# Head sums on quarters of TensorE, fixed orders in the key stage, and matrix exchanges ahead of the weight loads

## The chip, the cores and the metric

The kernel runs on one core of one Trainium2 chip. The metric is the device time of one execution in microseconds (us); lower is better. The figure for a kernel is the median of its runs.

## The reference

The program is a small decoder trunk of two layers: RWKV-7 time mixing, then gated linear attention, each followed by a squared-ReLU MLP. The width is 2048, there are 272 tokens (16 learned ones and 256 of the sequence), and everything is float32. Cut to the part that the change touches, the time mixing computes

```python
xr, xw, xk, xv, xa, xg = (x + xx * mix[i] for i in range(6))   # xx: previous token minus x
r, k, v = xr @ w_rkv[0], xk @ w_rkv[1], xv @ w_rkv[2]
w_log = -softplus(-(w0 + tanh(xw @ w1) @ w2)) - 0.5
a = sigmoid(a0 + (xa @ a1) @ a2)
kk = heads(k * k_k)                                            # 32 heads of 64
kk = kk / max(sqrt(sum(kk * kk, axis=-1)), 1e-12)              # sum over the head
k = k * (1 + (a - 1) * k_a)
decay = exp(-exp(w_log))
y = rwkv7_scan(r, decay, k, v, -kk, kk * a)                    # S <- S diag(w) + (S a) b^T + v k^T
bonus = sum(r * k * r_k, axis=-1) * v                          # sum over the head
```

The scan is carried out in chunks of 64 tokens. Inside a chunk it needs a 64x64 matrix of scores for each head and the inverse of a triangular matrix made from it.

## The kernel before

Activations lie with the 2048 channels on 16 tiles of 128 partitions and the 272 tokens along the free dimension. A projection onto one output tile f (0 to 15) multiplies 16 weight blocks of 128x128 with the 16 input tiles. To keep float32 accuracy, each weight and each input is split into a high and a low part, and a block takes three matmuls (`mm3`, L163 to L165). Weights arrive in half tiles of 128x1024 (`raw`, 512 KB, L132, on the SP queue); ScalarE makes `hi` (L140) and VectorE `lo` (L141). There are three `raw` buffers and two each of `hi` and `lo`. A scheduler orders the instructions of each engine by priority; weight loads are raised by 2000 places, so that they are issued well ahead.

The stages around the change, in the order of the program:

- **Low-rank stage** (`lora`, from L470). For each f it computes two tiles: the running sum of the decay, and a. It stores both (`ca`, 272 KB) in a scratch tensor in DRAM, `cad`.
- **Key stage** (the loop from L567). For each f: the projection `ps`; `ca` is read back; ScalarE makes exp(-) and exp(+) of the decay sum (`W` L574, `iW` L575), `kk` (L576), its square `sq` (L577), and the factor for `kn` (L578). TensorE sums `sq` over each head by a 128x128 matrix of ones on two diagonal blocks (`bones`, L580), ScalarE takes the inverse root (L581, L582), and VectorE makes the tiles `bk` and `ar` of products with W and iW. They go to DRAM (`bkd`, `ard`, 288 KB each). A second product with `bones` (L595) sums `kn` for the bonus, and ScalarE copies the result to `r` (L596). VectorE copies the last decay of each chunk to `WC` (L597) and the column without a decay at the head of each chunk of `ar` (L586). At f = 0 the input tiles of the value projection are mixed (L332 and after) on VectorE.
- **Scores and inversion.** `bk` and `ar` of eight tiles (16 heads) are fetched from DRAM when f is 7. `scores` (L525, and the masks on VectorE into `AM`) is called after f = 10 to 13. The triangular systems are written to DRAM (`sysd`, L531), read back in another layout (`sysA`, L549), inverted by 30 steps of two VectorE operations (`upd`, `sysA`) and four transposes (L561), written out (`invd`, L559), and read into `AM` (L565). The inversion of the first batch starts after f = 13. There are four batches, 0 to 3.
- **Recurrence.** After the key stage the value projection and others run, with the chunk recurrence between them. `merge` (L658) completes the inverses of a batch and needs `AM` from `invd`. Batches 1 to 3 are scored and inverted between these projections, and merged later.
- From about 600 us on the output projections, the MLP and the second layer run, which the change doesn't touch.

Of the kernel before, what the change touches and what calls it, by code (L numbers as in the profile page):

```python
# [11 lines left out]
F32R = mybir.dt.float32r  # L12
# [42 lines left out]
class Kern:  # L55
# [242 lines left out]
    def rwkv(self, done):  # L298
# [171 lines left out]
        def lora(f):  # L470
            l2 = self.t(e2, [96, 2, P], "l2", 3)
            nc.sync.dma_start(l2, ap["lora2"][f])
            st = self.t(ep, [P, 2, T], "ca", 2)
# [22 lines left out]
        Wf = self.t(ep, [P, T + 1], "W")  # L496
        nc.gpsimd.memset(Wf[:, 0:1], 1.0)
        W = Wf[:, 1:]

        def put(dst, slot, a, b, skip=0):  # L500
            v = dst[:, :512].rearrange("q (c s t) -> q c s t", c=4, s=2)[:, :, slot]
            tt(v, a[:, : 4 * C].rearrange("q (c t) -> q c t", c=4), b[:, : 4 * C].rearrange("q (c t) -> q c t", c=4))
            o = 512 + 32 * slot
            tt(dst[:, o + skip : o + 16], a[:, 4 * C + skip :], b[:, 4 * C + skip :])

# [9 lines left out]
        def scores(b, c, e):  # L515
            BK, AR = BKs[c > 1], ARs[c > 1]
            n, np = (C, 4) if c < NC4 else (32, 8)
            o = 128 * (c % 2) if c < NC4 else 256
            cs = slice(o, o + 2 * n)

            pv = [self.ptr().rearrange("p (h m) -> p h m", h=np)[: 2 * n, :, : 2 * n] for _ in range(2)]
            for p in range(np):
                for q in range(2):
                    rows = slice(64 * q, 64 * q + 64)
                    nc.tensor.matmul(pv[q][:, p], BK[rows, 4 * e + p, cs], AR[rows, 4 * e + p, cs], start=True, stop=True)  # L525
            dst, mk = (AMs[c > 1][:, c % 2, 8 * e : 8 * e + 8], self.maskA) if c < NC4 else (AMrs[0], self.maskR)
            for q in range(2):
                tt(dst[:, q::2], pv[q], mk.unsqueeze(1).to_broadcast([2 * n, np, 2 * n]))

            for rows, x in blocks(c, slice(8 * e, 8 * e + 8) if c < NC4 else slice(16)):  # L530
                nc.sync.dma_start(sysd[b][rows].rearrange("h s t -> s h t"), x)  # L531

        def blocks(c, heads):
            if c == NC4:
# [7 lines left out]
        def invert(b):  # L542
            X = sysA
            n = P if b % 2 else 64
            some_rows = [slice(0, 64), slice(96, 112)][: 1 + b % 2]
            if b % 2:
                nc.gpsimd.memset(X[64:96], 0.0)
            for rows in some_rows:
                nc.sync.dma_start(X[rows], sysd[b][rows])  # L549
            nc.gpsimd.memset(X[:n].rearrange("p a b -> p (a b)")[:, ::33], 1.0)  # L550
            yield
            for s in range(1, 31):
                k, m = 31 - s, s
                w = self.t(lp, [P, 256], "upd", 1)[:n, : k * m].rearrange("p (a b) -> p a b", a=m)
                tt(w, X[:n, s : s + 1, s + 1 :].to_broadcast([n, m, k]), X[:n, :m, s : s + 1].to_broadcast([n, m, k]))
                tt(X[:n, :m, s + 1 :], X[:n, :m, s + 1 :], w, ALU.add)
                yield
            for rows in some_rows:
                nc.sync.dma_start(invd[b][rows], X[rows])  # L559
            for k in (slice(8 * i, 8 * i + 8) for i in range(4)):  # L560
                nc.vector.transpose(t11.rearrange("p c h s -> p s c h")[:, k], X[0:32, k])  # L561
                yield
            for c in ((2, 3, 4) if b % 2 else (0, 1)):
                for rows, x in reversed(blocks(c, slice(0, 16))):
                    nc.sync.dma_start(x, invd[b][rows].rearrange("h s t -> s h t"))  # L565

        for f in range(KT):  # L567
            r = rr[f]
            bk, ar = st2[0][f % 2], st2[1][f % 2]
            ps = self.proj(pair(wk, f), xk, T, bank=self.pry if f % 3 == 2 else None)  # L570
            ca = self.t(ep, [P, 2, T], "ca", 2)
            nc.sync.dma_start(ca.rearrange("p a t -> p (a t)"), cad[f])
            iW, kk, sq, kn = (self.t(ep, [P, T], n, 2) for n in ("iW", "kk", "sq", "kn"))
            nc.scalar.activation(W, ca[:, 0], AF.Exp, scale=-DECAY)  # L574
            nc.scalar.activation(iW, ca[:, 0], AF.Exp, scale=DECAY)  # L575
            nc.scalar.mul(self.two(kk), ps, self.vec("k_k", f))  # L576
            nc.scalar.activation(sq, kk, AF.Square)  # L577
            nc.scalar.activation(kn, ca[:, 1], AF.Identity, scale=self.vec("k_a", f), bias=self.omka[:, f : f + 1])  # L578
            ss = self.pm()[:, :T]
            nc.tensor.matmul(ss, self.bones, sq, start=True, stop=True)  # L580
            nc.scalar.activation(sq, ss, AF.Ln, bias=self.tiny)  # L581
            nc.scalar.activation(sq, sq, AF.Exp, scale=-0.5)  # L582
            tt(self.two(kn), ps, self.two(kn))
            nc.vector.scalar_tensor_tensor(out=kk, in0=sq, scalar=1e12, in1=kk, op0=ALU.min, op1=ALU.mult)
            put(ar, 0, kk, Wf[:, :T], 1)
            nc.vector.tensor_copy(ar[:, 0:513:128], kk[:, ::C])  # L586
            tt(kk, kk, ca[:, 1])
            put(bk, 1, kk, iW)
            put(bk, 0, kn, iW)
            nc.sync.dma_start(bkd[f], bk)  # L590
            nc.vector.scalar_tensor_tensor(out=kn, in0=r, scalar=self.vec("r_k", f), in1=kn, op0=ALU.mult, op1=ALU.mult)
            put(ar, 1, r, W)
            nc.sync.dma_start(ard[f], ar)
            rk = self.pu()[:, :T]
            nc.tensor.matmul(rk, self.bones, kn, start=True, stop=True)  # L595
            nc.scalar.copy(r, rk)  # L596
            nc.vector.tensor_copy(WC[:, f], W[:, C - 1 : 4 * C : C])  # L597
            if f == 0:
                xv = mix(3, self.xp)
                early2.close()  # L600
                wl = ExitStack()
                lp = wl.enter_context(tc.tile_pool(name="wl", bufs=1, reuse_waits="tile"))
                BKs, ARs = ([self.t(lp, [P, 8, 256], n)] for n in ("BK0", "AR0"))
                AMs, AMrs = [self.t(lp, [P, 2, 16, 128], "AM0")], []
                sysA = self.t(lp, [P, 32, 32], "sysA")
                t11 = sysA.rearrange("p a b -> p (a b)")[64:96].rearrange("p (c h s) -> p c h s", c=2, h=16)
                nc.gpsimd.memset(sysA, 0.0)
            if f == 7:
                fetch(0, BKs, bkd)
                fetch(0, ARs, ard)  # L610
            if 9 < f < 14:
                scores(0, (f - 10) // 2, f % 2)
            if f == 13:
                inv = invert(0)
            if f > 13:
                for _ in range(6):
                    next(inv, None)
# [4 lines left out]
        BKs.append(self.t(kp, [P, 8, 320], "BK1"))  # L622
# [269 lines left out]
        units1 = ((2, 0), (2, 1), (3, 0), (3, 1), (4, 0))  # L892
        self.split_parts = 2
        for i in ((0, 128), (128, 320)):
            fetch(1, BKs, bkd, i)
            fetch(1, ARs, ard, i)
        ahead()
        with tc.manual_schedule(engines={mybir.EngineType.PE}):
# [423 lines left out]
```

## Time and profile before

| | us |
|---|---|
| median of 3 runs | 2404.45 (2400.09, 2404.45, 2407.26) |
| profiled execution | 2402.54 |
| its span | 2400.8 |
| TensorE busy | 2360.9 |
| VectorE busy | 1611.9 |
| ScalarE busy | 1242.4 |
| GpSimd busy | 6.6 |

The span runs from the first to the last instruction that the profiler saw. Busy is the time in which an engine had an instruction under way; what is missing to the span is idle. A row of a timeline gives the start, the duration, the engine, the line of the program and the operation with its output and input tiles, and in brackets the time for which the engine sat idle and what ended it. A row of a table by windows gives for a stretch of the span the busy time of TensorE, of its weight loads (PEld), VectorE (DVE), ScalarE (ACT) and GpSimd (POOL), then the granted clock of TensorE, the share of the DMA engines and the rate.

### The profile page before, as it was taken

What the parts mean: (1) busy time and instruction counts of PE and PEld (TensorE: products, weight loads), DVE (VectorE), ACT (ScalarE), POOL (GpSimd) and SP (SyncE); (2) the same over time, 40 slices, a digit from 0 to 9 for tenths busy, and PEclk for the clock granted to TensorE, in tenths of its full rate; (3) what the DMA queues carried; (4) which work ended last, traced back from release to release, by engine and by line L of the source; (5) the groups of instructions that cost most, each with busy time, mean ns of one, the idle gap of its engine ahead of it and who ended that gap; (6) DMA issues with size and microseconds to landing.
All of it is one profiled execution on the core that took longest, in us unless ns stands there. A gap on an engine that the chain in (4) does not pass through costs nothing. (4 is left out here: it accounts for less than half of the span.)

```text
span 2400.8 us, 48047 instructions
## 1 busy us (share of the span) xinstructions
PE 2360.9 (98%) x19689; PEld 2244.1 (93%) x19689; DVE 1611.9 (67%) x2734; ACT 1242.4 (52%) x1975; POOL 6.6 (0%) x20
## 2 busy tenths in 40 slices
PE   9999999899999999999999999999999999999998
PEld 8888888889999999999999999999999999999997
DVE  8777886858655555555556777767666666666666
ACT  6376644556555445445345556555555445445444
POOL 0000000000000000000000000000000000000000
PEclk9999999999999999999999999999999999999999
DMA  6578864524555555555555554455555555555554
GB/s 210 169 235 293 248 190 146 146 83 163 183 187 193 187 191 191 188 193 186 192 189 190 196 181 167 159 176 193 182 201 200 200 201 200 202 202 202 201 201 169
DMA packets 160732, 455.34 MB, mean 190 GB/s; under 512 B 34112, under 2 KB 50624, under 8 KB 160512
## 3 DMA queue, kind: packets, MB, share of 16 engines
q1 hardware_dynamic: 160512, 452.27, 55.8%
q8 instruction: 154, 2.52, 0.4%
q14 instruction: 66, 0.54, 0.1%
HBM read 433.86 MB, written 18.35 MB: 188 GB/s over the span
## 5 line engine op out<-in xcount | busy, mean ns | idle before, releaser
L141 DVE TENSOR_TENSOR lo<-raw,hi 128x1024 fp32r<-128x1024 f32 (+1 forms) x818 | 927.4, 1140 | 534.1 <-ACT hi L140 525.9
L140 ACT CAST hi<-raw 128x1024 fp32r<-128x1024 f32 (+1 forms) x818 | 794.6, 979 | 939.4 <-PE pj L164 546.8
L163 PE MATMUL pj<-x,hi 128*128 128x272 f32 (+1 forms) x2624 | 748.6, 285 | 1.7 <-DVE hres L300 1.0
L165 PE MATMUL pj<-x,lo 128*128 128x272 f32 (+1 forms) x2624 | 734.5, 280 | 4.3 <-DVE lo L141 4.1
L164 PE MATMUL pj<-x,hi 128*128 128x272 f32 (+1 forms) x2624 | 734.0, 280 | 0.2 <-DVE x L240 0.2
L163 PEld LDWEIGHTS pj<-x,hi 128*128 128x128 f32 x2624 | 498.1, 190 | 10.2 <-issue 3.7
L165 PEld LDWEIGHTS pj<-x,lo 128*128 128x128 f32 x2624 | 498.2, 190 | 7.2 <-DVE lo L141 6.5
L164 PEld LDWEIGHTS pj<-x,hi 128*128 128x128 f32 x2624 | 498.2, 190 | 3.6 <-issue 1.4
L196 PE MATMUL pj<-x,hi 128*128 128x512 f32 x1280 | 419.9, 382 | 0.1
L197 PE MATMUL pj<-x,lo 128*128 128x256 f32 x1280 | 348.8, 273 | 0.0
L196 PE MATMUL pj<-h,hi 128*128 128x512 f32 x1008 | 330.3, 382 | 0.0
L163 PE MATMUL pj<-h,hi 128*128 128x272 f32 (+1 forms) x1040 | 290.1, 279 | 0.0
L164 PE MATMUL pj<-h,hi 128*128 128x272 f32 (+1 forms) x1040 | 290.1, 279 | 0.0
L165 PE MATMUL pj<-h,lo 128*128 128x272 f32 (+1 forms) x1040 | 290.1, 279 | 0.0
L197 PE MATMUL pj<-h,lo 128*128 128x256 f32 x1008 | 274.8, 273 | 0.0
L196 PEld LDWEIGHTS pj<-x,hi 128*128 128x128 f32 x1280 | 241.9, 189 | 34.1 <-DVE x L996 0.4
L197 PEld LDWEIGHTS pj<-x,lo 128*128 128x128 f32 x1280 | 245.7, 192 | 0.3 <-DVE lo L141 0.2
L196 PEld LDWEIGHTS pj<-h,hi 128*128 128x128 f32 x1008 | 190.5, 189 | 26.5
L163 PEld LDWEIGHTS pj<-h,hi 128*128 128x128 f32 x1040 | 196.6, 189 | 0.0
L164 PEld LDWEIGHTS pj<-h,hi 128*128 128x128 f32 x1040 | 196.6, 189 | 0.0
L165 PEld LDWEIGHTS pj<-h,lo 128*128 128x128 f32 x1040 | 196.6, 189 | 0.0
L197 PEld LDWEIGHTS pj<-h,lo 128*128 128x128 f32 x1008 | 193.5, 192 | 0.0
(270 smaller groups left out, 2077.2 us busy)
## 6 DMA issues: line engine op xcount, KB each, us to landing
raw<-mlp_w_d SPq DMA_DIRECT2D x512, 512.0 KB, 3.3
raw<-gla_in_d SPq DMA_DIRECT2D x98, 512.0 KB, 3.2
raw<-w_rkv_d SPq DMA_DIRECT2D x80, 512.0 KB, 3.9
raw<-gla_o_d SPq DMA_DIRECT2D x32, 512.0 KB, 4.3
raw<-w_r_d SPq DMA_DIRECT2D x16, 512.0 KB, 3.3
raw<-rw_oQ_d SPq DMA_DIRECT2D x16, 512.0 KB, 3.2
ard<-ar SPq DMA_DIRECT2D x16, 288.0 KB, 3.4
bkd<-bk SPq DMA_DIRECT2D x16, 288.0 KB, 3.5
```

Source lines behind the costliest of these rows:

```text
L140: nc.scalar.copy(hi[:, h], raw[:, h])
L141: nc.vector.tensor_tensor(out=lo[:, h], in0=raw[:, h], in1=hi[:, h].bitcast(F32), op=ALU.subtract)
L163: nc.tensor.matmul(out, hi[:, ws], xh, start=first, stop=False)
L164: nc.tensor.matmul(out, hi[:, ws], xl, start=False, stop=False)
L165: nc.tensor.matmul(out, lo[:, ws], xh, start=False, stop=last)
L196: nc.tensor.matmul(wide, hi[:, ws], xt, start=kt == 0, stop=False)
L197: nc.tensor.matmul(one, lo[:, ws], xt[:, 0], start=False, stop=kt == nk - 1)
```

## The change

- **Head sums.** The two products with `bones` become four products of 64x64 for each f, on quarters of the array. `sq` goes through the two diagonal quarters. `kn` goes through the two others, so that its sums come out with the halves swapped; two copies of ScalarE put them right (before: one copy). All four are issued together in the middle of the next projection, `sq` of tile f-1 and `kn` of f-2.
- **Orders.** TensorE's order in the key stage is the program's. VectorE's products for `bk`, `ar`, `kk` and `kn` keep the program's order among themselves.
- **Low-rank tiles.** `ca` of f = 0 to 7 stays in SBUF, in slices of `hres`. Those of 8 to 15 go to `cad` as before and are loaded into a slice when the tile 8 places earlier is used up.
- **Decays.** `W` has a one at the head of each chunk (65 columns for a chunk) and two buffers. The 16 copies L586 are gone; the 16 copies to `WC` are on GpSimd.
- **Value inputs.** The 16 mixes (L332) of the value projection run in the low-rank stage, in place in `d`. Their split into high and low parts stays at the head of the key stage.
- **Stores and fetches.** Of the tiles f = 4 to 7, `store` sends the parts that the first batches need straight to `BK0`, `AR0` and `BK1` in SBUF. Tiles 0 to 3 are fetched at f = 5, 6 and 7. The two later fetches into `BK1` are gone.
- **Scores and inversion** each begin one projection earlier.
- **Exchanges.** The DMAs of `sysd`, `sysA`, `invd` and `AM` are raised by 4000 places, above the weight loads.

```diff
-            nc.sync.dma_start(cad[f], st.rearrange("p a t -> p (a t)"))
+            if f >= NR:
+                nc.sync.dma_start(cad[f], st.rearrange("p a t -> p (a t)"))
...
+            if f == KT - 2:
+                for kt in range(KT):
+                    mixed(d[:, kt], kt, 3)
...
             for rows in some_rows:
-                nc.sync.dma_start(invd[b][rows], X[rows])
+                with tc.high_priority(offset=4000):
+                    nc.sync.dma_start(invd[b][rows], X[rows])
...
-                    nc.sync.dma_start(x, invd[b][rows].rearrange("h s t -> s h t"))
-
-        for f in range(KT):
...
-            ss = self.pm()[:, :T]
-            nc.tensor.matmul(ss, self.bones, sq, start=True, stop=True)
...
-            put(ar, 0, kk, Wf[:, :T], 1)
-            nc.vector.tensor_copy(ar[:, 0:513:128], kk[:, ::C])
...
-            rk = self.pu()[:, :T]
-            nc.tensor.matmul(rk, self.bones, kn, start=True, stop=True)
-            nc.scalar.copy(r, rk)
-            nc.vector.tensor_copy(WC[:, f], W[:, C - 1 : 4 * C : C])
...
+        def store(f, dst, x, i):
+            q = nc.sync
+            if 3 < f < 8:
+                q.dma_start((BKs, ARs)[i][0][:, f], x[:, :256])
+                q.dma_start(dst[f][:, 256:] if i else BKs[1][:, f], x[:, 256:])
+            else:
+                q.dma_start(dst[f], x)
...
+            for x, out, i in todo:
+                for q in range(2):
+                    nc.tensor.matmul(out[half(q ^ i)], self.bones[half(q), half(q)], x[half(q)], start=True, stop=True)
+            if last:
+                for q in range(2):
+                    nc.scalar.copy(r[half(q)], rk[half(1 - q)])
...
+        with tc.manual_schedule(engines={ENG.PE}):
+            for f in range(KT + 1):
+                if f < KT:
+                    ps = (self.pry if f % 3 == 2 else self.pj)()[:, :T]
+                    keyproj(f, ps, 0)
+                if f:
+                    rest(f - 1)
+                if f < KT:
+                    keyproj(f, ps, 1)
+                    front(f, ps)
...
+                if 8 < f < 13:
+                    scores(0, (f - 9) // 2, (f + 1) % 2)
+                if f == 12:
+                    inv = invert(0)
+                if f > 12:
+                    for _ in range(6):
+                        next(inv, None)
+            sums(None)
```

TensorE before, around the head sums of tile f = 2 (`sq_2142` and `kn_2143`) in the projection f = 3 (`pj_2172`); the rows are line, operation, output and inputs, size:

```order
L165 MATMUL pj_2172<-x_1208,lo_2176 128x272
L163 MATMUL pj_2172<-x_1209,hi_2175 128x272
L580 MATMUL pm_2149<-sq_2142,cst_125 128x272
L164 MATMUL pj_2172<-x_1209,hi_2175 128x272
...
L165 MATMUL pj_2172<-x_1216,lo_2206 128x272
L595 MATMUL pu_2168<-kn_2143,cst_125 128x272
L163 MATMUL pj_2172<-x_1217,hi_2205 128x272
```

TensorE after the change, in the middle of the projection f = 3 (now `pj_2112`):

```order
L164 MATMUL pj_2112<-x_1212,hi_2115 128x272
L165 MATMUL pj_2112<-x_1212,lo_2116 128x272
L604 MATMUL pm_2147<-sq_2109,cst_125 64x272 x2
L604 MATMUL pu_2148<-kn_2048,cst_125 64x272 x2
L163 MATMUL pj_2112<-x_1213,hi_2176 128x272
L164 MATMUL pj_2112<-x_1213,hi_2176 128x272
```

The sums of `sq` (f = 2) and of `kn` (now f = 1) stand together between the two halves of the projection, as 2 and 2 matmuls of 64 rows; they stood apart, one of them within an `mm3`.

VectorE before, from the first product of f = 4 on:

```order
L300 TENSOR_TENSOR kn_2333<-pj_2267,kn_2333 128x272
L300 TENSOR_TENSOR bk_1788<-kn_2333,iW_2330 128x4x64
L300 TENSOR_TENSOR bk_1788<-kn_2333,iW_2330 128x16
L591 SCALAR_TENSOR_TENSOR kn_2333<-r_19_93,vecs_126,kn_2333 128x272
L584 SCALAR_TENSOR_TENSOR kk_2331<-sq_2332,kk_2331 128x272
L300 TENSOR_TENSOR ar_1790<-kk_2331,W_1796 128x4x64
L300 TENSOR_TENSOR ar_1790<-kk_2331,W_1796 128x15
L586 COPY ar_1790<-kk_2331 128x5
L141 TENSOR_TENSOR lo_2461<-raw_2458,hi_2460 128x1024
L300 TENSOR_TENSOR kk_2331<-kk_2331,ca_2328 128x272
L300 TENSOR_TENSOR ar_1791<-r_20_94,W_1796 128x4x64
L300 TENSOR_TENSOR bk_1788<-kk_2331,iW_2330 128x4x64
```

VectorE after, from the first product of f = 3 on:

```order
L300 TENSOR_TENSOR kn_2240<-pj_2112,kn_2240 128x272
L300 TENSOR_TENSOR bk_1789<-kn_2240,iW_2239 128x4x64
L300 TENSOR_TENSOR bk_1789<-kn_2240,iW_2239 128x16
L300 TENSOR_TENSOR ar_1791<-r_18_92,W_1797 128x4x64
L300 TENSOR_TENSOR ar_1791<-r_18_92,W_1797 128x16
L641 SCALAR_TENSOR_TENSOR kn_2240<-r_18_92,vecs_126,kn_2240 128x272
L141 TENSOR_TENSOR lo_2308<-raw_2305,hi_2307 128x1024
L643 SCALAR_TENSOR_TENSOR kk_2204<-sq_2205,kk_2204 128x272
L300 TENSOR_TENSOR ar_1791<-kk_2204,W_1797 128x4x64
L300 TENSOR_TENSOR ar_1791<-kk_2204,W_1797 128x16
L300 TENSOR_TENSOR kk_2204<-kk_2204,hres_72 128x272
L300 TENSOR_TENSOR bk_1789<-kk_2204,iW_2239 128x4x64
```

Each tile now has two groups (`bk` of kn, `ar` of r and the product for the bonus, then everything with the normalised `kk`), with one `lo` between them; the copies L586 and L597 are not there.

SP's queue before, from the store of the inverses of batch 2 on (`AM_402` is the buffer that the merge of that batch reads):

```order
L559 DMA invd_13_87<-sysA_1980 64x1024
L549 DMA sysA_1980<-sysd_10_84 16x1024
L132 DMA raw_5956<-rw_oQ_d 128x1024
L132 DMA raw_6058<-rw_oQ_d 128x1024
L565 DMA AM_402_1979<-invd_13_87 32x16x32
L132 DMA raw_6151<-rw_oQ_d 128x1024
L565 DMA AM_402_1979<-invd_13_87 32x16x32 x2
L132 DMA raw_6254<-rw_oQ_d 128x1024
L565 DMA AM_402_1979<-invd_13_87 32x16x32
L549 DMA sysA_1980<-sysd_10_84 64x1024
```

SP's queue after, from the same store on:

```order
L574 DMA invd_13_87<-sysA_2014 64x1024
L563 DMA sysA_2014<-sysd_10_84 16x1024
L132 DMA raw_5944<-rw_oQ_d 128x1024
L581 DMA AM_387_2013<-invd_13_87 32x16x32 x4
L563 DMA sysA_2014<-sysd_10_84 64x1024
L132 DMA raw_6046<-rw_oQ_d 128x1024
L132 DMA raw_6139<-rw_oQ_d 128x1024
L132 DMA raw_6242<-rw_oQ_d 128x1024
```

The four loads of `AM` now stand together, with one weight load between the store and them, and the loads of `raw` that stood among them stand behind.

More of the change, by code (lines that the diff above doesn't have):

```diff
@@ L564, in invert @@
                 for rows, x in reversed(blocks(c, slice(0, 16))):
-                    nc.sync.dma_start(x, invd[b][rows].rearrange("h s t -> s h t"))
-        for f in range(KT):
[L568 to L575, printed above, removed]
+                    with tc.high_priority(offset=4000):
+                        nc.sync.dma_start(x, invd[b][rows].rearrange("h s t -> s h t"))
@@ L579, in rwkv, with rest @@
-            ss = self.pm()[:, :T]
-            nc.tensor.matmul(ss, self.bones, sq, start=True, stop=True)
+            tiles[f] = ps, kk, sq
+        def rest(f):
+            r, W = rr[f], Wfs[f % 2]
+            bk, ar = st2[0][f % 2], st2[1][f % 2]
+            ps, kk, sq = tiles.pop(f)
+            i = f % NR
+            ca = hres[:, 2 * i : 2 * i + 2]
+            iW, kn = (self.t(ep, [P, T], n, 2) for n in ("iW", "kn"))
+            nc.scalar.activation(kn, ca[:, 1], AF.Identity, scale=self.vec("k_a", f), bias=self.omka[:, f : f + 1])
+            keep(tt(self.two(kn), ps, self.two(kn)))
+            ss = sums(sq)
+            nc.scalar.activation(W.rearrange("p (c t) -> p c t", c=5)[:, :, 1:],
+                                 ca.rearrange("p a t -> p (a t)")[:, : 5 * C].rearrange("p (c t) -> p c t", c=5),
+                                 AF.Exp, scale=-DECAY)
+            nc.scalar.activation(iW, ca[:, 0], AF.Exp, scale=DECAY)
@@ L608, in rwkv @@
[L608 to L617, printed above, removed]
+            put(bk, 0, kn, parts(iW))
+            put(ar, 1, r, decay(W, 1))
+            keep(nc.vector.scalar_tensor_tensor(out=kn, in0=r, scalar=self.vec("r_k", f), in1=kn, op0=ALU.mult, op1=ALU.mult))
@@ new lines, in rest @@
+            held.append((r, kn))
+            keep(nc.vector.scalar_tensor_tensor(out=kk, in0=sq, scalar=1e12, in1=kk, op0=ALU.min, op1=ALU.mult))
+            put(ar, 0, kk, decay(W, 0))
+            store(f, ard, ar, 1)
+            keep(tt(kk, kk, ca[:, 1]))
+            put(bk, 1, kk, parts(iW))
+            if f < NR:
+                nc.sync.dma_start(ca.rearrange("p a t -> p (a t)"), cad[f + NR])
+            store(f, bkd, bk, 0)
+            nc.gpsimd.tensor_copy(WC[:, f], W[:, C : 4 * C1 : C1])
```

85 lines of the change are left out of this document (53 added, 32 removed).

## The prediction

> **What bounds the kernel now.** I read the page first.
>
> ```profile
> span 2400.8 us, 48047 instructions
> PE 2360.9 (98%) x19689; PEld 2244.1 (93%) x19689; DVE 1611.9 (67%) x2734; ACT 1242.4 (52%) x1975; POOL 6.6 (0%) x20
> PE pj L196 18%; PE pj L197 9%; DVE fin L1229 0%; PE pj L164 0%; PE pj L163 0%; PE pj L165 0%; PE pm L1224 0%; PE pm L255 0%; DVE hres L1229 0%; DVEq L1317 0%; ACT acc L231 0%; DVE hres L213 0%; ACT acc L232 0%; ACT sq L1216 0%
> ```
>
> TensorE is busy for 98% and leads the chain that ended last. Only 2400.8 - 2360.9 = 39.9 us of it are idle in the whole span. So there are three ways to save: take work off TensorE, remove one of its waits, or keep its clock up. What another engine saves is worth only what it frees of these. The view by windows splits the part that the change touches (columns: busy time of PE, PEld, DVE, ACT, POOL, then the granted clock, DMA share and rate).
>
> ```profile
> 80.00:157.60 77.60, 76.43 (x468) 66.67 (x467) 48.27 (x84) 39.36 (x78) 0.00 (x0) 1.00 0.63 209
> 157.60:185.00 27.40, 25.64 (x199) 24.11 (x198) 26.36 (x69) 21.24 (x43) 0.96 (x1) 1.00 0.73 241
> 185.00:235.00 50.00, 47.60 (x364) 44.71 (x362) 40.17 (x102) 36.47 (x68) 0.00 (x0) 1.00 0.87 292
> 235.00:278.50 43.50, 41.27 (x325) 37.73 (x326) 36.12 (x98) 26.44 (x54) 0.00 (x0) 1.00 0.83 253
> 278.50:324.40 45.90, 43.00 (x380) 41.04 (x379) 43.75 (x118) 19.56 (x40) 0.15 (x1) 1.00 0.76 243
> 324.40:333.10 8.70, 7.67 (x86) 7.17 (x85) 6.96 (x12) 2.56 (x5) 0.00 (x0) 1.00 0.76 203
> ```
>
> The first row is the low-rank stage, the next three are the key stage, the fifth is the inversion of batch 0 beside the value projection, and the last reaches to the first merge. TensorE is idle for 10.3 us from 157.6 to 333.1. VectorE has 96% in the first stretch of the key stage and 95% while it inverts; there it is as good as full.
>
> **The head sums.** The timeline of one steady projection shows what they take.
>
> ```profile
> 200.63 0.28 PE L165 MATMUL pj<-x,lo 128*128 128x272 f32 x1
> 201.04 0.72 PE L580 MATMUL pm<-sq,cst 128*128 128x272 f32 x2
> 201.40 0.48 PE L163 MATMUL pj<-x,hi 128*128 128x272 f32 x1
> 201.72 0.28 PE L164 MATMUL pj<-x,hi 128*128 128x272 f32 x1
> ...
> 202.64 0.28 PE L163 MATMUL pj<-x,hi 128*128 128x272 f32 x1
> 202.76 0.28 PE L164 MATMUL pj<-x,hi 128*128 128x272 f32 x1
> 202.88 0.72 PE L595 MATMUL pu<-kn,cst 128*128 128x272 f32 x2
> 203.25 0.48 PE L165 MATMUL pj<-x,lo 128*128 128x272 f32 x1
> 203.56 0.28 PE L163 MATMUL pj<-x,hi 128*128 128x272 f32 x1
> ...
> 208.03 0.73 PE L580 MATMUL pm<-sq,cst 128*128 128x272 f32 x2
> ```
>
> A step of `mm3` takes 0.115 to 0.12 us (202.64 to 202.76), so 48 of them take 5.55 us. The projection takes 208.03 - 201.04 = 6.99 us. The two sums thus cost 1.44 us: 200.63 to 201.72 is 1.09 for two steps and a sum (0.86 for the sum), 202.76 to 203.56 is 0.80 (0.57 for the sum). The change replaces them by four matmuls on quarters. Before has no such matmul of 272 columns, but quarters appear in the recurrence.
>
> ```profile
> 397.46 0.27 PE L722 MATMUL pu<-S,AR 64*64 64x64 f32 x1
> 397.47 0.27 PE L720 MATMUL pry<-AR,S 64*64 64x64 f32 x1
> 397.48 0.27 PE L722 MATMUL pu<-S,AR 64*64 64x64 f32 x1
> 397.49 0.27 PE L720 MATMUL pry<-AR,S 64*64 64x64 f32 x1
> 397.57 0.22 PE L722 MATMUL pu<-S,AR 64*64 64x64 f32 x1
> ```
>
> Four start within 0.03 us of each other and the next four follow after 0.11: four quarters run at once. Below, the four sums could cost what the cheaper whole one costs now, 0.57 us. Above, if nothing overlaps, they cost four times 0.72, 2.9 us. The rows of quarters are the nearest, so I take 0.7 (0.57 and some for the turn between shapes, of which the 0.86 shows that there is one). That saves 0.74 x 16 = **11.8 us** of TensorE's work; 14 at best, and a loss of 23 at worst.
>
> The Trainium skill speaks against it in TensorEngine Tiling (Array Packing), Key Properties: "Mode switching requires drain", and the same page under Gotcha 1 has it that different row tiles cannot use one PSUM bank at once, which the two diagonal quarters of one output tile would do. By these the four would run in turn, at the 2.9 us above. The trace disagrees on the second: the rows of L720 and L722 share two banks, and start together.
>
> **The waits for `sq` and `kn`.** The waits of TensorE from 155 to 300 us:
>
> ```profile
> PE pm L580 <- ACT sq L577: 3.8, 5, 1.7
> PE pu L595 <- DVE kn L591: 2.0, 3, 1.7
> ```
>
> With the sums in mid-projection, `sq` has half a projection (2.8 us) to be made and `kn` more than one, so the 3.8 + 2.0 = **5.8 us** go. What is late next is ScalarE: its work per projection is now 36.47/50 x 6.99 = 5.1 us and grows by about 0.4 (one copy more, and the wider exp), to 5.5 of some 6.3. VectorE has 40.17/50 x 6.99 = 5.6, and loses its two small copies:
>
> ```profile
> L332 DVE SCALAR_TENSOR_TENSOR xm<-d,vecs,hnp 128x272 f32<-128x272 f32 x8 | 3.8, 497 | 0.0
> L597 DVE COPY WC<-W 128x4 f32<-128x4 f32 x15 | 2.4, 163 | 0.0
> L586 DVE COPY ar<-kk 128x5 f32<-128x5 f32 x14 | 2.4, 168 | 0.0
> ```
>
> That leaves 5.6 - 0.33 = 5.3 us. Both stay below 6.3 but have little room, and TensorE, VectorE and ScalarE are tied in one order: ss, then Ln, the two copies of `r`, exp, the second group of VectorE, a `lo`, the next first group. A DMA adds to this: at 292 GB/s a projection of 6.99 us moves 2.04 MB. The same in 6.3 us would be 324 GB/s and a share of 0.97, and eight stores and eight loads of 272 KB out of 16 and 16 fall away only in part of this stretch. I charge **+2 us** for exchanges and late `raw` (0 to 11.8, that is, all of the sums' gain).
>
> **The mixes.** Eight mixes of 0.497 us leave the window 157.6 to 278.5, and 16 enter the low-rank stage, where VectorE is idle for 77.60 - 48.27 = 29.3 us and TensorE leads. I put that at nothing; without the cover it would be 8 us. The gain in the first stretch, where VectorE has 96%, is in the 5.8 us above.
>
> **Where the gain meets the inversion.** From 157.6 to 333.1 VectorE has 26.36 + 40.17 + 36.12 + 43.75 + 6.96 = 153.4 us of work. It loses 3.8 + 2.4 + 2.4, and keeps 144.8. At the 95% that it reached while inverting, these need 152.4 us of the 175.5: room for a gain of 23. TensorE's own room is 11.8 and the 10.3 idle, 22.1. So neither alone forbids the gain, but the inversion now starts a projection earlier, so that one key tile more meets it, and each `lo` queues behind its chained operations on VectorE. The row 278.5 to 324.4, where the two met before, has 2.9 us of TensorE idle already. The tile more brings 5.3 us of VectorE's work to an engine at 95%: I take **+6 us** of new stalls, that work and a little for the exchange of `sysA`, which VectorE now waits for in the middle of its products. It is 0 at best (the room of 23 is used) and 12 at worst (two tiles' work).
>
> **The merges.** TensorE's waits from 300 to 620 us, the longer one in the timeline, the windows at the two merges, and SP's timeline at the second:
>
> ```profile
> PE pt L658 <- DMA AM<-invd: 4.4, 2, 3.5
> ```
> ```profile
> 453.46 1.27 PE L658 MATMUL pt<-AM,rs 32*32 32x32 f32 x39 [3.49 <-DMA AM<-invd]
> ```
> ```profile
> 376.00:380.00 4.00, 3.11 (x83) 2.82 (x78) 0.32 (x1) 1.62 (x5) 0.00 (x0) 1.00 1.05 294
> 380.00:384.00 4.00, 4.00 (x66) 3.75 (x68) 1.65 (x3) 2.45 (x6) 0.00 (x0) 0.57 0.13 24
> ...
> 452.00:456.00 4.00, 2.54 (x65) 2.47 (x66) 0.00 (x0) 1.31 (x4) 0.00 (x0) 0.51 0.79 221
> 456.00:460.00 4.00, 4.00 (x23) 3.90 (x22) 0.82 (x4) 0.15 (x1) 0.16 (x1) 0.63 0.55 139
> ```
> ```profile
> 446.23 0.38 SPq L565 DMA_DIRECT2D AM<-invd  x1
> 447.59 0.33 SPq L132 DMA_DIRECT2D raw<-rw_oQ_d  x1
> 447.95 0.97 SPq L565 DMA_DIRECT2D AM<-invd  x2
> 451.89 0.35 SPq L132 DMA_DIRECT2D raw<-rw_oQ_d  x1
> 452.30 0.42 SPq L565 DMA_DIRECT2D AM<-invd  x1
> ```
>
> The four loads are spread over 6 us because each `raw` between them waits for a free buffer. Issued together from 446.23 they are out by about 448, and the 4.4 us of waits should go. Behind each wait the clock falls to 0.5 to 0.6: 4 x 0.43 = 1.7 us lost at 380, and 4 x 0.49 x 2.54/4 + 4 x 0.37 = 2.7 at 452. Whether the drop goes with the wait the trace doesn't show, since small matmuls stand there too. Of 8.8 us I take **6** (0 to 8.8). The `raw` that now stand behind lose some 2 us, and `lo` lies two half projections ahead.
>
> The Trainium skill, in TensorE: Matmul & The Clock Gate, Part 1, puts the half clock down to an idle window of some 3.4 us; the stall of 3.49 us agrees; the other one, 4.4 - 3.5 = 0.9 us, is shorter, and the clock fell behind it too.
>
> **Sum**, against the profiled execution: 2402.5 - 11.8 - 5.8 + 2 + 6 - 6 = 2386.9, so **2387 us**. The profiled execution lies 1.9 below the median of 2404.45, which I leave in the uncertainty.
>
> **Rivals.**
>
> 1. *All of it arrives*: sums at 0.57, no new stalls or lateness, both merges in full. 2402.5 - 14 - 5.8 - 8.8 = 2374 us. For it: room on VectorE for 23. Against: VectorE's 95% in the inversion.
> 2. *The quarters overlap only in part* and cost what the sums cost now, 1.44: 2402.5 - 5.8 + 6 + 2 - 6 = 2398.7 us; the stalls would then be fewer too, down to 2394. For it: the turn between shapes is unseen for this width.
> 3. *Another engine or the DMA sets the pace* of the key stage, and a projection stays at 6.99: the sums' gain and that of the waits are lost, and only the merges remain, 2402.5 - 6 = 2396.5 us. For it: the DMA share of 0.87 and ScalarE's 5.5 us in one fixed chain. Against: the fixed order leaves TensorE half a projection of cover.
> 4. *Slower: the quarters run in turn.* The skill's rules above would do this. At 2.9 us for four, each projection gets 1.46 longer, 23.4 in all; the waits go (-5.8), VectorE has time (no stalls), the merges gain 6: 2402.5 + 23.4 - 5.8 - 6 = 2414 us. It is slower than can be told from no change once the four cost 2.8 or more. Against: the rows of L720 and L722.
>
> **Chances.** The forecast 0.47, rival 1 0.20, rival 2 0.13, rival 3 0.13, rival 4 0.07. A difference of about 0.3% (7.2 us, so 2397.2 to 2411.7) is what a measurement can tell from no change. Faster: the forecast, rival 1, and half of rival 3, about 0.74. Within: rival 2 and the other half of 3, 0.19. Slower: 0.07. The forecast's own range is 2380 to 2394. The range that reaches to rivals 1, 2 and 3 is 2373 to 2402.
>
> **What would show it.** In the profile of the changed kernel, the sums' row should have four starts within 0.1 us and the projections a period of 6.2 to 6.4 us; the waits for `sq` and `kn` should be gone. The key stage should end some 12 us earlier, and the first merge about 10 (11.8 + 5.8 - 2 - 6). TensorE should wait for `lo` in the inversion for about 6 us more than now. The waits L658 should be below 1 us, and the clock in the windows behind them nearer to 1. I am wrong if the period stays near 7 with `lo` or `raw` late (rival 3), if the starts of the quarters lie 0.3 us or more apart (2 or 4), or if the clock drops without a wait (the merges then give 4.4).

## The result and the profile after

| | before | after |
|---|---|---|
| median, us | 2400.88 (6 runs, 2400.09 to 2407.26) | 2385.49 (6 runs, 2384.69 to 2386.64) |
| span of the profiled execution, us | 2400.8 | 2382.6 |
| TensorE busy, us | 2360.9 | 2349.0 |

The ratio is 0.9932, with a 95% interval of 0.992 to 0.9944: the change is faster by 15.4 us. The prediction was 2387 us. The median of before over six runs is 3.6 us lower than that over the first three.

From the page after:

```profile
PE 2349.0 (99%) x19753; PEld 2231.2 (94%) x19753; DVE 1608.1 (67%) x2702; ACT 1251.8 (53%) x1995; POOL 12.4 (1%) x37
```

The span is 18.2 us shorter. TensorE has 11.9 us less of work (slow clock counts as work here, and so do waits that hide behind a matmul's end, of which more below) and 6.3 us less idle time (33.6 after 39.9).

The key stage after, by windows (the columns as in the prediction):

```profile
157.60:185.00 27.40, 27.40 (x235) 25.44 (x238) 22.68 (x50) 21.85 (x43) 2.02 (x4) 1.00 0.75 247
185.00:235.00 50.00, 49.12 (x439) 43.91 (x440) 44.65 (x107) 40.03 (x79) 2.50 (x7) 1.00 0.92 313
```

TensorE has 0.9 us of idle time in these 77.4 us; before it had 4.2. The DMA share has risen to 0.92. One set of head sums after, in the timeline of TensorE:

```profile
204.10 0.28 PE L165 MATMUL pj<-x,lo 128*128 128x272 f32 x1
204.45 0.45 PE L604 MATMUL pm<-sq,cst 64*64 64x272 f32 x2
204.46 0.45 PE L604 MATMUL pu<-kn,cst 64*64 64x272 f32 x2
204.73 0.40 PE L604 MATMUL pm<-sq,cst 64*64 64x272 f32 x2
...
205.07 0.38 PE L163 MATMUL pj<-x,hi 128*128 128x272 f32 x1
```

The quarters start within 0.01 us of each other, in two passes 0.28 us apart. Ahead of them 0.35 us pass from the last matmul of the projection, where a step otherwise takes 0.12. Most of the difference is a wait. TensorE's weight loads (PEld) show it, and so does ScalarE:

```profile
203.98 0.42 ACT L620 ACTIVATE sq<-kk 128x272 f32<-128x272 f32 x1
204.45 0.14 PEld L604 LDWEIGHTS pm<-sq,cst 64*64 64x64 f32 x2 [0.28 <-ACT sq L620]
```

`sq` is ready at 204.40, and the weight load and the quarters begin at 204.45. In a later projection, where `sq` has been ready for 1.02 us, only 0.21 us pass:

```profile
233.35 0.28 PE L165 MATMUL pry<-x,lo 128*128 128x272 f32 x1
233.56 0.45 PE L604 MATMUL pm<-sq,cst 64*64 64x272 f32 x2
...
234.18 0.38 PE L163 MATMUL pry<-x,hi 128*128 128x272 f32 x1
234.40 0.28 PE L164 MATMUL pry<-x,hi 128*128 128x272 f32 x1
```

Without a wait, four quarters thus cost 234.40 - 233.35 - 0.23 = 0.82 us. (The 0.23 are the two ordinary steps in that time; the same sum is used below.)

The next set after that at 204.45 starts 7.26 us later, where `sq` is late by more; the steady period is 6.52 us. So the sums cost 6.52 - 5.55 = 0.97 us in the steady projections, 0.14 of it a wait, where they cost 1.44 before. TensorE could go faster: the first two periods are 6.37 us, and `sq` is ready 0.89, 0.49, 0.15 and then 0.05 us ahead of the first four sets. From then on the period is 6.52, and `sq` comes just in time. ScalarE works without a gap from `W` at 201.97, which had waited 0.99 us for VectorE, up to `sq`. So here TensorE follows the chain of ScalarE and VectorE.

TensorE's waits after, from 150 to 290 us:

```profile
PE pu L604 <- DVE kn L641: 2.5, 1, 2.5
PE pm L604 <- ACT sq L620: 1.9, 3, 0.9
PE pj L163 <- ACT hres L884: 1.4, 1, 1.4
```

Where the gain arises and goes can be read from ScalarE's copies of the value projection's eight results (`hres`, one for each tile). Before, the first, fourth and eighth:

```profile
287.87 0.38 ACT L816 COPY hres<-pj 128x272 f32<-128x272 f32 x1
...
306.58 0.38 ACT L816 COPY hres<-pj 128x272 f32<-128x272 f32 x1
...
339.72 0.39 ACT L816 COPY hres<-pj 128x272 f32<-128x272 f32 x1
```

After, the same three:

```profile
274.29 0.38 ACT L884 COPY hres<-pj 128x272 f32<-128x272 f32 x1
...
300.74 0.38 ACT L884 COPY hres<-pj 128x272 f32<-128x272 f32 x1
...
330.90 0.39 ACT L884 COPY hres<-pj 128x272 f32<-128x272 f32 x1
```

The changed kernel is 13.6 us ahead at the first value tile, only 5.8 at the fourth, and 8.8 at the eighth. Most of the loss in between is the crowded VectorE. The last sum of `kn` stands in TensorE's fixed order two value tiles behind the key stage, and its `kn` is late all the same, since 17 steps of the inversion stand before it on VectorE. In the windows, the wait of 2.5 us and the clock behind it:

```profile
280.00:284.00 4.00, 1.50 (x12) 0.89 (x11) 4.00 (x13) 1.38 (x3) 0.00 (x0) 1.00 0.25 75
284.00:288.00 4.00, 4.00 (x23) 4.00 (x22) 3.60 (x11) 0.91 (x3) 0.00 (x0) 0.57 0.54 165
```

VectorE is full. With 1.4 us (bank not yet freed by the copy at 274.29), 2.5, 1.7 of slow clock and 1.7 for the fetch of `AR` at 295, this stretch costs 7.3 us.

At the second and third merge the changed kernel doesn't wait, and the clock stays up:

```profile
368.00:372.00 4.00, 4.00 (x122) 3.70 (x124) 0.76 (x2) 2.71 (x8) 0.00 (x0) 1.00 0.40 139
...
440.00:444.00 4.00, 4.00 (x39) 3.58 (x38) 1.36 (x7) 1.92 (x6) 0.00 (x0) 1.00 0.54 189
```

### The profile page after: what moved, and what is told of

Read it like the earlier page. It is cut to its first block, busy times and chain, and to the rows that moved or that the text cites. A ratio compares the mean times of both kernels' runs of the same rounds, so it can differ in the third digit from the quotient of the medians.

```text
span 2382.6 us, 48158 instructions
## 1 busy us (share of the span) xinstructions
PE 2349.0 (99%) x19753; PEld 2231.2 (94%) x19753; DVE 1608.1 (67%) x2702; ACT 1251.8 (53%) x1995; POOL 12.4 (1%) x37
## 5 line engine op out<-in xcount | busy, mean ns | idle before, releaser
L163 PEld LDWEIGHTS pj<-x,hi 128*128 128x128 f32 x2624 | 497.6, 190 | 17.1 <-issue 8.4
```

The lines of the kernel that those rows point to most:

```text
L163: nc.tensor.matmul(out, hi[:, ws], xh, start=first, stop=False)
```

## The experiments

### Whole sums in the new place

```diff
-                for q in range(2):
-                    nc.tensor.matmul(out[half(q ^ i)], self.bones[half(q), half(q)], x[half(q)], ...)
+                nc.tensor.matmul(out, self.bones, x, start=True, stop=True)
```

> The changed kernel with the two head sums as whole 128x128 products again, in the new place. Theory (quarters save TensorE's work): the period of a steady key projection goes from 6.52 us to between 6.75 and 6.99, so 4 to 7.5 us more in all, about 2391. Rival (the new order is what gained, the quarters nothing): the period stays within 0.1 us of 6.52 and the time within 2 us of 2385.5.

Measured: 2383.67 us (2381.99 to 2385.02), ratio to before 0.9922 (0.9904 to 0.9941). The period is 6.52 us, the same as with quarters. The timeline of TensorE, in a steady projection and in a later one:

```profile
196.94 0.28 PE L165 MATMUL pj<-x,lo 128*128 128x272 f32 x1
197.05 0.67 PE L603 MATMUL pm<-sq,cst 128*128 128x272 f32 x2
...
198.13 0.28 PE L164 MATMUL pj<-x,hi 128*128 128x272 f32 x1
```
```profile
233.01 0.28 PE L165 MATMUL pry<-x,lo 128*128 128x272 f32 x1
233.12 0.62 PE L603 MATMUL pm<-sq,cst 128*128 128x272 f32 x2
...
234.16 0.28 PE L164 MATMUL pry<-x,hi 128*128 128x272 f32 x1
```

Two whole sums cost 198.13 - 196.94 - 0.23 = 0.96 us in the steady projection, where `sq` is ready 0.11 us ahead of them. In the later one, where it has been ready for 1.45 us, they cost 234.16 - 233.01 - 0.23 = 0.92. Against this the quarters' 0.82 saves 0.10 us, but only where `sq` is early; in the steady projections both kernels have the period that `sq` allows. In the kernel's time the quarters save nothing, and the theory that they were the gain falls. The rival stands: the gain is in the new order, of which the place of the sums is a part.

### Each sum twice

```diff
-            for x, out, i in todo:
+            for x, out, i in todo + todo:
```

This was run with quarters and with whole sums. The repeated products write the same results again.

> The changed kernel with the four quarter products of each projection issued twice (the second time over the same results). It measures what four quarters add without a further turn from the projection's shape and back. Theory (a turn costs about 0.48 us, and two quarters that read the same rows of the array take turns, so four quarters stream like two whole products, 0.48 us): the period goes from 6.52 to 7.0. Rival (all four run at once): to 6.76. Rival (all in turn): to 7.4 or more.

> The changed kernel with whole 128x128 sums, both issued twice. Theory (two whole products stream in 0.48 us, the rest of the 0.96 us is the turn): the period goes from 6.52 to 7.0, as with the quarters. Rival (whole products cost more than quarters and the first pair hides it): above 7.2.

Measured: 2396.34 us and a period of 7.43 with quarters, 2398.3 us and 7.83 with whole sums (one run each). With quarters, TensorE's timeline:

```profile
200.27 0.45 PE L604 MATMUL pm<-sq,cst 64*64 64x272 f32 x2 [0.53 <-ACT sq L620]
...
200.55 0.40 PE L604 MATMUL pm<-sq,cst 64*64 64x272 f32 x2
...
201.01 0.40 PE L604 MATMUL pm<-sq,cst 64*64 64x272 f32 x2
...
201.35 0.38 PE L163 MATMUL pj<-x,hi 128*128 128x272 f32 x1
```

Four more quarters took 200.55 to 201.01, two passes of 0.23: 0.46 us. The other half of the period's growth of 0.91 is a longer wait for `sq`: the first quarter starts 0.81 us behind the projection's last matmul (199.46), where it was 0.35. With whole sums:

```profile
203.35 0.62 PE L603 MATMUL pu<-kn,cst 128*128 128x272 f32 x2
203.81 0.62 PE L603 MATMUL pm<-sq,cst 128*128 128x272 f32 x2
```

In a row, a whole sum takes 0.46 us. So the theory behind both expectations was wrong too: a whole sum streams in 0.46 and not in 0.24. The 0.48 expected for four more quarters was nearly met, but for another reason: they don't take turns, they run at once and take as long as one whole sum. The quarters do halve the streaming (0.46 for 0.92). They give most of it back at their ends: of the 0.82 us that a set costs without a wait, 0.36 are spent going in and out, where two whole sums lose nothing (0.92).

### The sums apart, as quarters and whole

```diff
-            ..., held.pop() if held else None
+            ..., held.pop() if held and sq is None else None
...
                     keyproj(f, ps, 1)
+                    if f:
+                        sums(None)
```

> The changed kernel with the two kinds of quarter sums apart: those of sq in mid-projection, those of kn at the end of the projection. Theory (joining them saves a turn of 0.48 us): the period goes from 6.52 back to about 7.0, that of the kernel before, although all are quarters. Rival (quarters are what saved): the period stays at 6.5 to 6.6.

> Whole 128x128 sums apart, in the places of the run with quarters apart: sq in mid-projection, kn at the end. In the kernel before the sum of sq began 0.06 us after ScalarE had finished sq, so 0.3 of its 0.86 us was a wait that the list of waits leaves out. Theory (that hidden wait was most of what the new places save; a whole sum without it costs 0.57 us wherever it stands): the period is 5.56 + 1.14 = 6.70, less than the 7.16 with quarters apart, and the time about 2386 to 2388. Rival (a lone whole sum costs 0.7 or more at these places, joining alone saves): 6.95 to 7.0.

Measured: quarters apart, 2391.45 us and a period of 7.16; whole sums apart, 2387.76 us and 6.90 (one run each). The second kernel has the edit of the whole sums as well. With quarters apart:

```profile
200.19 0.28 PE L165 MATMUL pj<-x,lo 128*128 128x272 f32 x1
200.40 0.68 PE L604 MATMUL pm<-sq,cst 64*64 64x272 f32 x4
...
201.23 0.28 PE L164 MATMUL pj<-x,hi 128*128 128x272 f32 x1
```

Each pair of quarters costs 201.23 - 200.19 - 0.23 = 0.81 us, as much as the four joined do without a wait. So apart they are worse than the whole sums of the kernel before (1.62 us for 1.44), and joining them is what makes quarters as good as whole sums. For whole sums apart, ScalarE and TensorE show:

```profile
205.56 0.42 ACT L619 ACTIVATE sq<-kk 128x272 f32<-128x272 f32 x1
```
```profile
205.59 0.28 PE L165 MATMUL pj<-x,lo 128*128 128x272 f32 x1
206.03 0.73 PE L603 MATMUL pm<-sq,cst 128*128 128x272 f32 x2 [0.16 <-ACT sq L619]
...
209.25 0.28 PE L165 MATMUL pj<-x,lo 128*128 128x272 f32 x1
209.37 0.62 PE L603 MATMUL pu<-kn,cst 128*128 128x272 f32 x2
...
209.94 0.28 PE L164 MATMUL pry<-x,hi 128*128 128x272 f32 x1
```

The sum of `kn`, which waits for nothing, costs 209.94 - 209.25 - 0.23 = 0.46 us. The sum of `sq` starts 0.05 us after ScalarE has finished `sq` (205.98). From the step before it 0.44 us have passed, of which 0.32 are more than a step, though the row names only 0.16 as a wait. Without the 0.32 the period would be 6.58. So the place in mid-projection doesn't remove the wait by itself; in the run with whole sums together, `sq` was early enough. And 6.90 decides between the two expectations only with these rows. They say the same as the kernel before, on this row of ScalarE:

```profile
200.55 0.43 ACT L577 ACTIVATE sq<-kk 128x272 f32<-128x272 f32 x1
```

`sq` was ready at 200.98 and L580 began at 201.04, and so in every steady projection. Of its 0.86 us, 0.3 ahead of it were a wait that the list of the matmuls' waits didn't show, because the matmul ahead of it counts as busy until its modelled end. The weight loads of the kernel before show it, and a second one with VectorE's row for `kn`:

```profile
201.04 0.30 PEld L580 LDWEIGHTS pm<-sq,cst 128*128 128x128 f32 x2 [0.33 <-ACT sq L577]
202.33 0.50 DVE L591 SCALAR_TENSOR_TENSOR kn<-r,vecs,kn 128x272 f32<-128x272 f32 x1
202.88 0.30 PEld L595 LDWEIGHTS pu<-kn,cst 128*128 128x128 f32 x2
```

`kn` was ready at 202.83, and the weight load of its sum began at 202.88, together with its matmul. Where `kn` is old, as in the run with whole sums apart, the load begins 0.11 us ahead of the matmul, and the sum costs 0.46. The kernel before has such a sum too: L595 at 250.06, its `kn` ready 0.22 us before, cost 0.46. So 0.40 of the 0.86 us and 0.11 of the 0.57 were waits, 0.51 together, and what is left of the 1.44 is the 0.92 that two whole sums cost without a wait.

### Exchanges not raised

```diff
-                    with tc.high_priority(offset=4000):
+                    with ExitStack():
```

> The changed kernel without the raised priority of the DMAs of sysd, sysA, invd and AM. Theory (the raised exchange removed the waits and clock drops at the merges, 3.0 us at the second merge and 6.2 at the third): the waits for AM come back, and the time is about 9 us longer, 2394.7. Rival (the shorter key stage moved the merges to where their data had landed): the waits stay away and the time is within 2 us of 2385.5.

Measured: 2390.46 us (2389.32 to 2392.64), 5.0 more than the changed kernel. TensorE's waits from 300 to 620 us and the window behind:

```profile
PE pt L726 <- DMA AM<-invd: 3.4, 1, 3.4
```
```profile
440.00:444.00 4.00, 3.91 (x71) 3.84 (x72) 0.00 (x0) 1.45 (x4) 0.00 (x0) 0.51 1.03 269
```

The wait at the third merge comes back with its slow clock (0.51, and 0.63 in the next 4 us). That of 0.9 us at the second does not. The truth lies between theory and rival: raising the exchanges is worth the third merge, and at the second the other parts of the change are enough.

### The kernel before with only the exchanges raised

```diff
-                nc.sync.dma_start(invd[b][rows], X[rows])
+                with tc.high_priority(offset=4000):
+                    nc.sync.dma_start(invd[b][rows], X[rows])
```

(and so for `sysd`, `sysA` and `AM`)

> The kernel before with only the priority of the exchanges raised. Theory (the parts add up): the waits at the merges and the clock drops go, 8 to 9 us less than the kernel before, about 2392. Rival (it needs the earlier inversion as well): less than 3 us gained.

Measured: 2395.62 us (2393.55 to 2398.59), ratio 0.9974 (0.9965 to 0.9983). It gains 5.8 us, nearer to the theory. There is no wait for `AM` in its profile, at the second merge neither. It reaches the first merge 1.0 us later than the kernel before, which may have taken part of the gain.

### The inversion later

```diff
-                if f == 12:
+                if f == 13:
                     inv = invert(0)
-                if f > 12:
+                if f > 13:
```

> The changed kernel with the inversion of batch 0 begun after f = 13, as in the kernel before; the scores stay where they are. Theory (the inversion crowds VectorE and makes kn of the last tile late, 2.5 us of wait and a clock drop of 1.7 us behind it, while AM of batch 0 lands some 10 us ahead of its merge): 2 to 4 us less, about 2382.5. Rival (the early inversion is needed for the first merge): TensorE waits at the first merge and the time is 3 to 7 us longer.

Measured: 2382.2 us (2381.15 to 2383.09), ratio 0.9916 (0.9899 to 0.9934). Of TensorE's waits from 150 to 290 us:

```profile
PE pu L604 <- DVE kn L641: 0.2, 1, 0.2
```

The others are 2.0 us for the `kn` product (L300), 1.5 for `sq`, 1.0 for a `lo` and 0.4 in the low-rank stage. The wait for the last `kn` shrinks from 2.5 to 0.2 us, and the 3.3 us gained lie within what the theory gave. The first merge is reached 4.0 us earlier than in the changed kernel (323.0 after 327.0), and doesn't wait. The intervals of the two ratios overlap, but all four runs lie below the six of the changed kernel. So beginning the inversion earlier, a part of the change, cost time.

### Whole sums and the inversion later

Both edits above together.

> The changed kernel with whole sums and the inversion begun after f = 13, the two edits that each gave a shorter time (2383.7 and 2382.2). Theory (both only shorten stalls behind the key stage, whose room is the same): about 2381 to 2382, little better than the later inversion alone. Rival (the two add): 2380.4.

Measured: 2378.49 us (2378.19 to 2379.11), ratio to before 0.9898 (0.9882 to 0.9915). It is the fastest version here, 7.0 us below the changed kernel, and a little more than the sum of the two edits (1.8 and 3.3). Its ratio's interval lies below that of the changed kernel (0.992 to 0.9944). TensorE's waits from 150 to 290 us that are left are 1.2 us for the `kn` product (L300), 0.4 in the low-rank stage and two of 0.2.

### The mixes back in the key stage

```diff
-            if f == KT - 2:
-                for kt in range(KT):
-                    mixed(d[:, kt], kt, 3)
...
                     for kt in range(KT):
+                        mixed(d[:, kt], kt, 3)
                         hl(xv[kt], d[:, kt])
```

> The changed kernel with the 16 mixes of the value projection back at the head of the key stage. Theory (they are hidden in the low-rank stage and were not where they stood, as VectorE has 83% of the first stretch of the key stage now and would have 100% with 8 us more): TensorE waits in the first projections, 2 to 5 us more than 2385.5. Rival (VectorE has room and nobody waits): within 1.5 us.

Measured: 2385.68 us (2383.89 to 2386.89). The rival holds: in the new order moving the mixes is worth nothing that these runs can tell.

### VectorE's order free

```diff
         def keep(*a):
-            for x in a:
-                tc.keep_in_program_order(x)
+            pass
```

> The changed kernel with VectorE's order in the key stage left to the scheduler. Theory (TensorE's order and the sums' place make the period, VectorE has 5.8 of 6.5 us): within 2 us of 2385.5. Rival (the fixed order keeps kn and the lo in time): 3 us or more longer, with waits of TensorE for kn or lo.

Measured: 2392.69 us (2388.79 to 2394.59), ratio 0.9962 (0.9948 to 0.9976), 7.2 us more by the medians than the changed kernel. The profiled execution is the fastest of the five, at 2388.79, so its waits can stand for only some 3.3 of the 7.2. TensorE's waits from 150 to 320 us:

```profile
PE pm L603 <- ACT sq L619: 6.2, 10, 0.9
PE pj L165 <- DVE lo L141: 3.0, 3, 2.6
```

The rival holds. `sq` is late at ten of the sums although the sums haven't moved: without the kept order, VectorE takes its products in another sequence, and the chain that ends in `sq` takes longer.

### Low-rank tiles through DRAM

```diff
-            st = hres[:, 2 * f : 2 * f + 2] if f < NR else self.t(ep, [P, 2, T], "ca", 2)
+            st = self.t(ep, [P, 2, T], "ca", 2)
...
-            ca = hres[:, 2 * i : 2 * i + 2]
+            ca = self.t(ep, [P, 2, T], "ca", 2)
+            nc.sync.dma_start(ca.rearrange("p a t -> p (a t)"), cad[f])
```

The store to `cad` is made for all 16 tiles, and the loads eight places ahead are gone.

> The changed kernel with all 16 low-rank tiles through DRAM again, read back one by one as in the kernel before: eight stores more in the low-rank stage and eight loads of 272 KB more in the first half of the key stage. Theory (DMA bounds there: 313 GB/s at a share of 0.92 leaves room for 340, and 272 KB in 6.52 us are 43 more, 356): late raw, TensorE waits for lo, 2 to 4 us more. Rival (the deeper buffers absorb it): within 1.5 us of 2385.5.

Measured: 2404.51 us (2402.44 to 2406.68), ratio to before 1.0013 (1.0004 to 1.0022): 19 us more than the changed kernel, the whole gain and more. The bandwidth doesn't look like the reason, for the share of the DMA engines falls from 0.92 to 0.85 from 185 to 235 us. ScalarE's waits from 157.6 to 268 us:

```profile
ACT kn L630 <- DMA ca<-cad: 11.0, 6, 3.6
ACT W L633 <- DMA ca<-cad: 9.9, 3, 4.5
```

In the kernel before, ScalarE waited 5.2 us for `ca` in that stretch. Here it is 20.9. SP issues the load of `ca` behind the stores of `ar` and `bk`, which wait for VectorE, and the load takes 4.6 us to land (the median in that stretch). The casts, Ln and exp stand behind it on ScalarE. So the fixed order needs the tiles to be there early, which those kept in SBUF, and those loaded eight places ahead, are.

## Why the prediction was right

The time was met to 1.5 us. The sum was made against the profiled execution, and there it fell short: 15.6 us were predicted and the spans differ by 18.2. The steps behind it fared differently.

- **The sums: right sign, the term too large, and the wrong cause.** The prediction put four quarters at 0.7 us and the saving at 0.74 us a projection, 11.8 in all. Measured are 0.97 and 0.47, or 7.5 in 16 projections. The step that failed is "I take 0.7 (0.57 and some for the turn between shapes, of which the 0.86 shows that there is one)". The 0.86 shows no turn; 0.40 of it was a wait for `sq`, and 0.11 of the 0.57 one for `kn`. So of the 1.44 us only 0.92 were TensorE's work, and the quarters, at 0.82 without a wait, save 0.10 of it and not 0.74. What was gained is the wait, and whole sums in the new place gain it as well. It takes more than the place: with the whole sums apart, the sum of `sq` in mid-projection costs 0.89 us (205.59 to 206.71, less two steps), and with VectorE's order free a joined set of quarters costs 1.4 to 1.5 us in most projections where it costs 0.82 without a wait. Quarters overlap as the rows of L720 and L722 had suggested, but their ends cost most of what the overlap saves.
- **What sets the pace.** The prediction's sign was a period of 6.2 to 6.4 us. TensorE has 6.37 in the first projections, then 6.52, in step with `sq`. The prediction gave `sq` half a projection of time and yet saw that ScalarE and VectorE "have little room" and that the three engines "are tied in one order"; that chain now sets the steady period. This is the mechanism of its third rival, at 6.52 in place of the 6.99 that the rival gave.
- **The rule that spoke against it.** Without a wait, a set of quarters takes 0.36 us more than its streaming: 0.21 us from the projection's last matmul to the first pass, 0.33 from the last pass back to the projection, and 0.22 for the step after, where a step takes 0.12 and a pass 0.23. By the Trainium skill, TensorEngine Tiling (Array Packing), Key Properties, a change of tiling mode drains the array; the rows agree with it. Its Gotcha 1, that row tiles cannot use one bank at once, isn't borne out: the two quarters of `sq`, which write one bank, start in the same row. The time that the prediction gave for that rule, 2414, supposed that the quarters run in turn, and they don't.
- **The waits for `sq` and `kn`.** The 5.8 us were to go. The listed waits from 157.6 to 285 us sum to 7.2 us before and 1.9 after up to the end of the key stage, 5.3 less. The last `kn` waits 2.5 us, which the prediction's stalls hold. The waits that the list leaves out are in the term of the sums.
- **+2 us for exchanges and late `raw`.** No wait for `raw` shows on TensorE. With 13.6 us of lead at the first value tile, sums (7.5) and waits (5.3) make 12.8; there is no room for a loss of 2.
- **+6 us of new stalls.** The size was about right: 13.6 us of lead fall to 8.8 at the last value tile. But TensorE doesn't wait for `lo` there, as the prediction said it would; it waits for the last `kn`, a bank and `AR`. The later inversion shows that the cause was VectorE, as predicted.
- **-6 us at the merges.** From the last value tile to the first row of ScalarE behind the recurrence (L231, at 617.29 before and 600.17 after) the lead grows from 8.8 to 17.1 us, so the gain was 8.3. The waits and the clock drops both went, as the rival with everything arriving had it. Raising the exchanges alone gives 5.8 in the kernel before, and taking it out of the changed one costs 5.0; the rest belongs to the other parts. Another 1.1 us of lead come later, in the part that the change doesn't touch.
- **The mixes at nothing**: right, as the run with them back shows.
- **What was not costed.** The prediction gave the low-rank tiles in SBUF no term of their own. Undone, with each load just ahead of its use, the kernel takes 19 us more. They don't add to the gain so much as carry it: ScalarE's chain of the fixed order has no room for a late `ca`. The same holds for VectorE's kept order, 7.2 us, which the prediction hadn't costed either.

So the sum came out by luck, with errors of both signs: 4.3 us too much for the sums and 0.5 for the waits, against 2 too much for lateness, 1.2 too much for the stalls (4.8 measured), 2.3 too little for the merges, and 1.9 that no term holds (0.8 ahead of the first value tile, 1.1 behind the recurrence).

What stays open: whether the 1.8 us between quarters and whole sums are real (the intervals of the two ratios overlap), what made up these 1.9 us, and which link of the chain of ScalarE and VectorE holds the period at 6.52, for no run shortened one.

## What to carry to other kernels

A short wait can hide ahead of a matmul: when an instruction begins within 0.1 us of the end of its producer every time, and the step before it is longer than its neighbours or its weight load comes late, the excess is a wait and no cost of the instruction, whatever the list of the matmuls' waits says. To price an instruction, take a place where its operand is old. Move it to where its operand is older before making it smaller. Before a gain is put down to a part of a change, run that part undone alone; here the quarters in the title gave nothing in the kernel's time, and tiles kept in SBUF, which looked like a saving of bandwidth, held up the whole order.

## What the runs showed of the hardware

- Four f32 products of 64x64x272 on the four quarters run at once, in two passes of 0.23 us, as long as one 128x128x272 product (0.46 us). Between the projection's 128x128 matmuls, and with operands that were ready long before, a set of four cost 0.82 us, 0.36 more than its streaming, and two whole products 0.92. Alone, a pair of quarters cost 0.81 us and a whole product 0.46.
- The weight load of a matmul waits with it: with an operand that is old it begins 0.11 us ahead of the matmul, and with one that has just come, together with it, 0.05 us behind the producer (202.83 and 202.88). Late weight loads so lengthened a sum by 0.11 us without an idle time of the matmuls.
- The granted clock fell to 0.57 in the four microseconds behind a wait of 2.5 us, and to 0.51 and 0.63 behind one of 3.4. Behind waits of 1.4, 1.7 and 1.8 us in the changed kernel it stayed at 1.00. In the kernel before it fell to 0.57 behind a wait of 0.9 at the second merge, among small matmuls. A threshold can't be read from these.
